# Attention with value parts side by side: denominators summed on GpSimd, the mask of the maxima put into the keys' sums

## The chip, the cores and the metric

The kernel runs on one core of a Trainium2 chip. The metric is the device time of one execution in microseconds (us); three executions of the kernel before took 2696.48, 2701.54 and 2703.55 us. Engines are called TensorE (PE; PEld is its weight load), VectorE (DVE), ScalarE (ACT), GpSimd (POOL) and SyncE (SP, which issues the loads).

## The reference

A two-layer decoder trunk on one sequence of 1024 tokens of width 1024, in float32. Layer 0 mixes tokens by attention with a forget gate (8 heads of 64) and by causal pooling, layer 1 by a recurrent delta rule (RWKV-7); a SwiGLU feed-forward block of width 2816 follows each. The change touches only the attention:

```python
logits = (jnp.einsum('bhqd,bhkd->bhqk', q_i, k).astype(jnp.float32) * scale
          + c_i[..., :, None] - cum[..., None, :])
causal = key_pos[None, :] <= q_pos[:, None]
p = jax.nn.softmax(jnp.where(causal, logits, -1e30), axis=-1)
return jnp.einsum('bhqk,bhkd->bhqd', p.astype(v.dtype), v)
```

`cum` is the running sum of the logarithm of the forget gate, so each key carries a number that is subtracted from its logits. The output of each head is then multiplied by a sigmoid gate.

## The kernel before

Matmuls take float32 operands rounded to a shorter form (`F32R`). To keep float32 accuracy an operand is split into a high part, rounded, and a low part, the rest; a product is then three matmuls: high by high, high by low, low by high (`mm3`, L163 to L165). ScalarE copies the high part, VectorE subtracts for the low one.

Everything is held transposed: channels or keys on the 128 partitions, tokens along the row, in halves of 512 tokens. Heads go in four pairs `p`, two heads `a` per pair; a head's 64 channels lie on its `own` half of the partitions, the `oth` half is free for other uses. For each head there are three steps:

- `assemble` splits the head's keys and queries into `KA`, `QA`, `KB`, `QB` and transposes its values (L490) into the high part `VH` (ScalarE, L492) and the low part `VL` (VectorE, L493). `VH` and `VL` have 128 columns per block of 128 keys: 64 for the head's values, and 64 others that were set once on GpSimd to ones in `VH` and to zeros in `VL`.
- `maxima` finds, for each query, the largest logit, so that the exponentials stay in range. It loads `cum` of the head, spread over all partitions, into `bc` (L500). For each block of 128 queries `i` from 0 to 7 and each half of the keys it makes the scores (L509), adds the causal mask in the diagonal block by a matmul of the identity with `maskQR` (L511), and VectorE subtracts `bc` and takes the largest (L512). The results go into rows of `QB`.
- `attend` makes, for each half `hq` of the queries and each block `j` of keys, the scores (L538, L539, mask L541 in the diagonal block), the exponentials `pt` (ScalarE, L543), their high part `ph` (ScalarE, the helper at L121) and low part `pl` (VectorE, L547), and one step later the values: `VH` by `ph` (L556), `VH` by `pl` (L557), `VL` by `ph` (L558), summed in one PSUM tile `o`. Since 64 columns of `VH` are ones, the `oth` half of `o` is the sum of the exponentials, the softmax's denominator. After the last `j`, ScalarE takes its logarithm (L563), VectorE adds the gate's logarithm (L564), ScalarE takes the exponential of the negative (L565), and VectorE multiplies (L566). A half has 4 or 8 blocks; widths are 512 columns, and 384, 256, 128 for the diagonal blocks that follow the first.

While a head is attended to, the next head is assembled and its maxima are found (`side`), and other matmuls fill TensorE: the projections of the next pair (`prep`), pooling units and gates, and for the last pair the output projection (`oproj_early`, which first splits 14 output tiles). `weave` interleaves these generators by the costs that they yield. A scheduler of the recording layer then sets each engine's order; each engine executes its own list in that order. Scratch tiles come from small rings: two PSUM tiles `s` for all scores, one `t`, two `o`, and five `tmp` tiles in SBUF that the pooling units, the heads' norms and the tail of `attend` share.

## Time and profile before

| | |
|---|---|
| median of 3 runs | 2701.54 us |
| profiled execution | 2699.03 us, its span 2697.2 us |
| TensorE busy, share of the span | 2633.8 us, 98% |
| VectorE | 1724.3 us, 64% |
| ScalarE | 1301.9 us, 48% |
| GpSimd | 50.6 us, 2% |
| first maxima to last values | about 72 to 466 us |
| two heads (pairs 0 to 2) | 101.3 us |

Busy time of TensorE is the union of matmuls that overlap: a 512-wide matmul lasts about 0.39 us in the records, and the next starts about 0.23 us after it. So the distance of starts, not the duration, is what a matmul costs. A stretch's bound is read from which engine has no idle time there and from what the others wait for.

### The profile page before, as it was taken

To read this page: it belongs to the slowest core of one execution; us is meant where nothing else is said; L and a number is where in the kernel's file an instruction comes from. 1 tells how busy PE (TensorE), PEld (TensorE's weight loads), DVE (VectorE), ACT (ScalarE), POOL (GpSimd) and SP (SyncE) were. 2 spreads that over 40 slices of the span, in tenths; PEclk is the share of its full clock that TensorE was granted. 3 is DMA by queue.
4 is the path that set the end of the run, shared out by engine and by line. 5 is a ranking of instruction groups with operands and counts; after the bars stand their busy time and mean duration, and the time that the engine had idled before them with its cause. 6 is when DMAs were issued, how large, how long until landed. Compare 5 with 4: busy or idle time off the path is not lost.

```text
span 2697.2 us, 40269 instructions
## 1 busy us (share of the span) xinstructions
PE 2633.8 (98%) x15368; PEld 2080.5 (77%) x15368; DVE 1724.3 (64%) x2940; ACT 1301.9 (48%) x2299; POOL 50.6 (2%) x139
## 2 busy tenths in 40 slices
PE   8999999999999999999999999999999999999999
PEld 6787878788888777777777677777777778888887
DVE  8777684654446655975995685469768856634443
ACT  7555564442224765534634466664445444332232
POOL 1000000000001000000000000000000000000000
PEclk9999999999999999999999999999999999999999
DMA  4111131233333546424523534454344336333333
GB/s 136 58 52 55 44 98 48 83 97 96 96 98 114 168 162 191 129 82 123 160 87 100 194 101 161 160 182 128 91 141 134 93 100 199 109 98 94 98 98 94
DMA packets 170817, 307.03 MB, mean 114 GB/s; under 512 B 18928, under 2 KB 25968, under 8 KB 170624
## 3 DMA queue, kind: packets, MB, share of 16 engines
q1 hardware_dynamic: 156800, 279.29, 33.6%
q10 hardware_dynamic: 13824, 25.17, 2.5%
q8 instruction: 120, 1.97, 0.3%
q14 instruction: 73, 0.60, 0.1%
HBM read 257.96 MB, written 46.43 MB: 113 GB/s over the span
## 4 chain that ended last, share of the span: by engine, by line
PE 77%; DVE 14%; DMA 3%; ACT 3%; issue 2%; SPq 0%; DVEq 0%; ACTq 0%
PE mm L163 16%; PE mm L164 16%; PE mm L165 16%; PE fm L163 6%; PE fm L164 5%; PE fm L165 5%; DVE wlo L152 2%; PE mm L175 1%; DVE nu L1108 1%; DVE pd L1106 1%; DMA wraw<-in_wu_dram 1%; DVE ZL L1064 1%; ACT whi L151 1%; PE o L1173 1%; PE s L1161 1%
## 5 line engine op out<-in xcount | busy, mean ns | idle before, releaser
L151 ACT CAST whi<-wraw 128x512 fp32r<-128x512 f32 x738 | 453.7, 617 | 867.4 <-PE mm L164 478.7
L152 DVE TENSOR_TENSOR wlo<-wraw,whi 128x512 fp32r<-128x512 f32 x738 | 501.3, 684 | 449.6 <-ACT whi L151 441.1
L163 PE MATMUL mm<-hh,whi 128*128 128x512 f32 x864 | 344.1, 400 | 6.2 <-ACT hh L355 6.1
L165 PE MATMUL mm<-hh,wlo 128*128 128x512 f32 x864 | 338.4, 392 | 0.0
L164 PE MATMUL mm<-hl,whi 128*128 128x512 f32 x864 | 337.9, 392 | 0.0
L163 PE MATMUL mm<-uh,whi 128*128 128x512 f32 x728 | 283.6, 391 | 0.9 <-DVE x L1317 0.9
L165 PE MATMUL mm<-uh,wlo 128*128 128x512 f32 x728 | 283.1, 390 | 1.0 <-DVE wlo L152 1.0
L164 PE MATMUL mm<-ul,whi 128*128 128x512 f32 x728 | 283.2, 390 | 0.0
L163 PE MATMUL fm<-h1h,whi 128*128 128x512 f32 x528 | 220.2, 417 | 14.8 <-DVE sg L726 9.9
L164 PE MATMUL fm<-h1l,whi 128*128 128x512 f32 x528 | 210.3, 398 | 0.1
L165 PE MATMUL fm<-h1h,wlo 128*128 128x512 f32 x528 | 209.5, 397 | 0.5 <-DVE wlo L152 0.5
L163 PEld LDWEIGHTS mm<-hh,whi 128*128 128x128 f32 x864 | 162.3, 188 | 43.4 <-ACT hh L355 7.8
L165 PEld LDWEIGHTS mm<-hh,wlo 128*128 128x128 f32 x864 | 162.5, 188 | 34.4 <-issue 0.2
L164 PEld LDWEIGHTS mm<-hl,whi 128*128 128x128 f32 x864 | 162.7, 188 | 33.1 <-DVE hl L260 1.7
L163 PE MATMUL fm<-hh,whi 128*128 128x512 f32 x416 | 170.9, 411 | 3.3 <-ACT hh L259 2.3
L164 PE MATMUL fm<-hl,whi 128*128 128x512 f32 x416 | 164.9, 396 | 0.2 <-DVE hl L260 0.2
L165 PE MATMUL fm<-hh,wlo 128*128 128x512 f32 x416 | 164.6, 396 | 0.0
L163 PEld LDWEIGHTS mm<-uh,whi 128*128 128x128 f32 x728 | 136.5, 188 | 34.6 <-issue 3.5
L164 PEld LDWEIGHTS mm<-ul,whi 128*128 128x128 f32 x728 | 136.6, 188 | 30.9 <-issue 1.1
L165 PEld LDWEIGHTS mm<-uh,wlo 128*128 128x128 f32 x728 | 136.7, 188 | 30.1 <-DVE wlo L152 1.8
L705 DVE TENSOR_TENSOR x<-mm,x 128x512 f32<-128x512 f32 x96 | 66.3, 692 | 119.3 <-PE mm L165 119.2
L163 PEld LDWEIGHTS fm<-h1h,whi 128*128 128x128 f32 x528 | 100.6, 191 | 47.1 <-DVE sg L726 12.2
(338 smaller groups left out, 4645.4 us busy)
## 6 DMA issues: line engine op xcount, KB each, us to landing
wraw<-in_wg_dram SPq DMA_DIRECT2D x176, 256.0 KB, 2.8
wraw<-in_wu_dram SPq DMA_DIRECT2D x176, 256.0 KB, 2.7
wraw<-in_wd_dram SPq DMA_DIRECT2D x176, 256.0 KB, 2.7
wraw<-in_w_in_dram SPq DMA_DIRECT2D x52, 256.0 KB, 2.9
x<-in_xT_dram SPq DMA_DIRECT2D x32, 256.0 KB, 4.6
x<-x SPq DMA_DIRECT2D x32, 256.0 KB, 3.3
wraw<-in_w_k_dram SPq DMA_DIRECT2D x32, 256.0 KB, 2.8
wraw<-in_w_v_dram SPq DMA_DIRECT2D x32, 256.0 KB, 3.0
```

The source lines that it names most:

```text
L151: k.nc.scalar.copy(hi[0:p, 0:n], raw[0:p, 0:n])
L152: k.nc.vector.tensor_tensor(lo[0:p, 0:n], raw[0:p, 0:n], rd(hi[0:p, 0:n]), ALU.subtract)
L163: nc.tensor.matmul(out, wh, xh, start=(first and i == 0), stop=False)
L164: nc.tensor.matmul(out, wh, xl, start=False, stop=False)
L165: nc.tensor.matmul(out, wl, xh, start=False, stop=(last and i == n - 1))
L175: k.nc.tensor.matmul(out[n * q:n * q + n], w[:, n * j:n * j + n], xs[j], start=c == 0, stop=c + g == len(xs), tile_position=(0, n * q))
L705: nc.vector.tensor_tensor(X[half][m], o, X[half][m], ALU.add)
L1064: nc.vector.tensor_tensor(ZL[h][HS[1 - h], i, bs], s4[HS[1]], self.msk[HS[1]].rearrange("p a t -> p (a t)").unsqueeze(1).broadcast_to([64, ...
L1106: nc.vector.tensor_tensor(pv, nu[:, j + 1:32, j:j + 1].broadcast_to([P, n, j]), nu[:, j:j + 1, 0:j].broadcast_to([P, n, j]), ALU.mult)
L1108: nc.vector.tensor_tensor(nu[:, j + 1:32, 0:j], nu[:, j + 1:32, 0:j], pv, ALU.add)
L1161: nc.tensor.matmul(z[HS[h], i], ZL[h][:, i, c, 0:64], SV[h][:, i, c], start=True, stop=True)
L1173: nc.tensor.matmul(sp[HS[h], i], BK[h][:, i, c], uv[h][:, i], start=True, stop=True)
```

## The change

Four things change.

- `VH` holds both parts side by side: the head's 64 `own` columns are the high part, the 64 `oth` columns the low part (VectorE writes it there). `VL` and the fills with ones and zeros are gone. Two matmuls remain per step, `VH` by `ph` and by `pl`; the `oth` half of `o` now holds the low part's products, and the two halves must be added at the end.
- The denominators: the exponentials of block `j = 0` are written into a tile `da`; for every further `j` GpSimd adds `pt` to it. At the end of a half, `finish` splits the sum into two parts (`part`: copy on ScalarE, subtraction on VectorE), copies the low half of `o` on ScalarE and adds it to the other half on VectorE, and then sums over the keys by two matmuls of `onesR` (all 1/64) with the two parts. Logarithm, gate, exponential and product follow as before. The tail takes four `tmp` tiles in place of one, and yields in two places, so that other work is woven in between.
- The maxima's mask matmuls are gone. GpSimd subtracts the mask from the diagonal block in `bc`, in place, so that the reduction on VectorE includes it.
- As the masked block stays masked, the blocks of queries go from the last to the first. `bc` has 512 more columns, a second copy of the first half of `cum` by a second load, so that query blocks 0 to 3 are masked there while blocks 4 to 7 read the unmasked first half.

```diff
-        nc.vector.tensor_tensor(VL[a][:, :, own], pvb, rd(VH[a][:, :, own]), ALU.subtract)
+        nc.vector.tensor_tensor(VH[a][:, :, oth], pvb, rd(VH[a][:, :, own]), ALU.subtract)
...
-        bc = ap_.tile([P, S], F32, tag="bc", name=nm(k, "bc"), bufs=1)
-        nc.sync.dma_start(bc, cumd[h:h + 1, :].broadcast_to([P, S]))
+        bc = ap_.tile([P, S + HN], F32, tag="bc", name=nm(k, "bc"), bufs=1)
+        nc.sync.dma_start(bc[:, 0:S], cumd[h:h + 1, :].broadcast_to([P, S]))
+        nc.sync.dma_start(bc[:, S:], cumd[h:h + 1, 0:HN].broadcast_to([P, HN]))
...
-        for i in range(8):
-            n = (i + 1) * P
-            for c in range(0, n, HN):
-                w = min(HN, n - c)
-                s = pst(k, "s", k.sbufs)
-                last = c + w == n
-                nc.tensor.matmul(s[:, 0:w], QA[a][:, P * i:P * i + P], KA[a][:, c:c + w], start=True, stop=not last)
-                if last:
-                    nc.tensor.matmul(s[:, w - P:w], identR, maskQR, start=False, stop=True)
-                nc.vector.tensor_tensor_reduce(s[:, 0:w], s[:, 0:w], bc[:, c:c + w], 1.0, -3e38, ALU.subtract, ALU.max,
-                                               mx[:, c // HN, i:i + 1])
-                yield w / HN + (0.5 if last else 0)
+        for i, c, at in [(i - d, c, at) for i in (7, 6, 5, 4) for d, c, at in ((0, HN, HN), (4, 0, S), (0, 0, 0))]:
+            w = min(HN, (i + 1) * P - c)
+            if at:
+                blk_ = bc[:, at + w - P:at + w]
+                nc.gpsimd.tensor_tensor(blk_, blk_, rd(maskQR), ALU.subtract)
+            s = pst(k, "s", k.sbufs)
+            nc.tensor.matmul(s[:, 0:w], QA[a][:, P * i:P * i + P], KA[a][:, c:c + w], start=True, stop=True)
+            nc.vector.tensor_tensor_reduce(s[:, 0:w], s[:, 0:w], bc[:, at:at + w], 1.0, -3e38, ALU.subtract, ALU.max,
+                                           mx[:, c // HN, i:i + 1])
+            yield w / HN + (0.5 if at else 0)
...
+            if j == 0:
+                pt = den[a, hq] = ap_.tile([P, HN], F32, tag="da", name=nm(k, "da"), bufs=2)
+            else:
+                pt = ap_.tile([P, HN], F32, tag="pt", name=nm(k, "pt"), bufs=2)
...
+            if j:
+                d = den[a, hq][:, q0 - hq * HN:]
+                nc.gpsimd.tensor_tensor(d, d, pt[:, 0:w], ALU.add)
...
-            nc.tensor.matmul(oo, VH[a][:, j], pl[:, 0:w], start=False, stop=False)
-            nc.tensor.matmul(oo, VL[a][:, j], ph[:, 0:w], start=False, stop=(j == nj - 1))
+            nc.tensor.matmul(oo, VH[a][:, j], pl[:, 0:w], start=False, stop=(j == nj - 1))
...
+            dh, dl = (ap_.tile([P, HN + 16], F32R, tag="tmp", name=nm(k, "dd"), bufs=k.tmpbufs)[:, 0:HN] for _ in range(2))
+            part(k, (dh, dl), d)
+            low = tmp("low")[:, 0:HN]
+            nc.scalar.copy(low[own], o[oth])
+            num = tmp("num")[:, 0:HN]
+            nc.vector.tensor_tensor(num[own], o[own], low[own], ALU.add)
+            yield 2
+            t = pst(k, "t", 1)
+            nc.tensor.matmul(t, onesR, dh, start=True, stop=False)
+            nc.tensor.matmul(t, onesR, dl, start=False, stop=True)
+            nc.scalar.activation(low[own], t[own], AF.Ln, scale=64.0)
+            nc.vector.tensor_tensor(low[own], low[own], y[p][hq][own], ALU.add)
+            nc.scalar.activation(low[own], low[own], AF.Exp, scale=-1.0)
+            nc.vector.tensor_tensor(y[p][hq][own], num[own], low[own], ALU.mult)
+            yield 0
...
             live.append(scores(*st))
             yield 2 * live[-1][4] / HN + 0.3
+            if ends and next(ends[0], None) is None:
+                ends.pop()
...
+        for e in ends:
+            yield from e
```

Three places in the engines' orders show what this moves. In these lists a line number is that of the kernel listed, so the change's numbers differ from the ones above: L537, L538 and L540 are its scores, L550 the low part `pl`, L553 the addition on GpSimd, L508 the mask on GpSimd, L562 and L563 the two value matmuls, L580 and L581 the two matmuls of `onesR`.

TensorE at the end of head 0, before: the last values, and the next head's first scores.

```order
L163 MATMUL mm_1268<-hh_392,whi_1219 128x512
L164 MATMUL mm_1268<-hl_393,whi_1219 128x512
L165 MATMUL mm_1268<-hh_392,wlo_1220 128x512
L556 MATMUL o_1072<-ph_1303,VH_109 128x128
L557 MATMUL o_1072<-pl_1304,VH_109 128x128
L558 MATMUL o_1072<-ph_1303,VL_111 128x128
L538 MATMUL s_1329<-QA_104,KA_102 128x512
L539 MATMUL s_1329<-QB_108,KB_106 128x512
L541 MATMUL s_1329<-maskTR,identR 128x128
```

The same place with the change (`dd` are the two parts of the denominators' sum):

```order
L165 MATMUL mm_1273<-hh_386,wlo_1226 128x512
L562 MATMUL o_1067<-ph_1308,VH_109 128x128
L563 MATMUL o_1067<-pl_1309,VH_109 128x128
L580 MATMUL t_1336<-dd_1326,onesR 128x512
L581 MATMUL t_1336<-dd_1327,onesR 128x512
L537 MATMUL s_1343<-QA_104,KA_102 128x512
L538 MATMUL s_1343<-QB_108,KB_106 128x512
L540 MATMUL s_1343<-maskTR,identR 128x128
```

The third product is gone, and the two matmuls of the denominators stand between the last values and the next head's scores, with no other matmul ahead of them. It is so for heads 0, 2 and 4.

VectorE at the same place with the change (`QA`, `KB`, `KA`, `QB` are assembly copies for a later head, `pl_1309` belongs to the last values above):

```order
L123 CAST KB_105<-ak_1135 64x512
L480 TENSOR_TENSOR KA_101<-ak_1135,KA_101 64x512
L484 TENSOR_TENSOR QB_107<-aq_1217,QA_103 64x512
L550 TENSOR_TENSOR pl_1309<-pt_1306,ph_1308 128x128
L260 TENSOR_TENSOR dd_1327<-da_1003,dd_1326 128x512
L441 TENSOR_TENSOR av_1334<-mm_1273,rs_98 128x512
L152 TENSOR_TENSOR wlo_1477<-wraw_1478,whi_1476 128x512
L577 TENSOR_TENSOR num_1332<-o_1067,low_1330 64x512
```

New are `dd_1327`, the low part of the sum, right behind the last `pl`, and `num_1332`, the addition of the two halves of `o`.

GpSimd with the change, during head 0, whose list held in this place only the small operations of the pooling units:

```order
L553 TENSOR_TENSOR da_838<-da_838,pt_981 128x128
L508 TENSOR_TENSOR bc_929<-bc_929,maskQR 128x128
L553 TENSOR_TENSOR da_1003<-da_1003,pt_1036 128x512
L508 TENSOR_TENSOR bc_929<-bc_929,maskQR 128x128 x2
L553 TENSOR_TENSOR da_1003<-da_1003,pt_1089 128x512
```

Additions for the head that is attended to and masks for the next head's maxima now take turns in one list.

More of the change, by code (lines that the diff above doesn't have):

```diff
@@ L381, in fox @@
     VH = [ap_.tile([P, 8, P], F32R, tag=f"VH{a}", name=f"VH{a}") for a in range(2)]
-    VL = [ap_.tile([P, 8, P], F32R, tag=f"VL{a}", name=f"VL{a}") for a in range(2)]
     for a in range(2):
@@ L388, in fox @@
         nc.gpsimd.memset(KB[a][64 - 64 * a:72 - 64 * a].bitcast(F32), 1.0)
-        nc.gpsimd.memset(VH[a][:, :, oth].bitcast(F32), 1.0)
-        nc.gpsimd.memset(VL[a][:, :, oth].bitcast(F32), 0.0)
     R = [K() for _ in range(4)]
@@ L395, in fox @@
     cumd = k.dram.tile([8, S], F32, tag="cum", name="cum")
-    cum = ap_.tile([P, S], F32, tag="bc", name="cum", bufs=1)[0:8]
+    cum = ap_.tile([P, S + HN], F32, tag="bc", name="cum", bufs=1)[0:8, 0:S]
     def forget(half, wf):
@@ L527, in attend @@
         steps = [(a, hq, j) for hq in range(2) for j in range(4 * hq + 4)]
-        live = []
-        out = {}
+        live, ends = [], []
+        out, den = {}, {}
         def scores(a, hq, j):
@@ L541, in scores @@
                 nc.tensor.matmul(s[:, 0:P], identR, maskTR, start=False, stop=True)
-            pt = ap_.tile([P, HN], F32, tag="pt", name=nm(k, "pt"), bufs=2)
+            if j == 0:
+                pt = den[a, hq] = ap_.tile([P, HN], F32, tag="da", name=nm(k, "da"), bufs=2)
+            else:
+                pt = ap_.tile([P, HN], F32, tag="pt", name=nm(k, "pt"), bufs=2)
             nc.scalar.activation(pt[:, 0:w], s[:, 0:w], AF.Exp, bias=ncumT[:, j, h:h + 1])
@@ L556, in values, with finish @@
             nc.tensor.matmul(oo, VH[a][:, j], ph[:, 0:w], start=(j == 0), stop=False)
-            nc.tensor.matmul(oo, VH[a][:, j], pl[:, 0:w], start=False, stop=False)
-            nc.tensor.matmul(oo, VL[a][:, j], ph[:, 0:w], start=False, stop=(j == nj - 1))
+            nc.tensor.matmul(oo, VH[a][:, j], pl[:, 0:w], start=False, stop=(j == nj - 1))
             if j == nj - 1:
-                own = slice(64 * a, 64 * a + 64)
-                oth = slice(64 - 64 * a, 128 - 64 * a)
-                den = tmp("den")[:, 0:HN]
-                nc.scalar.activation(den[own], o[oth], AF.Ln)
-                nc.vector.tensor_tensor(den[own], den[own], y[p][hq][own], ALU.add)
-                nc.scalar.activation(den[own], den[own], AF.Exp, scale=-1.0)
-                nc.vector.tensor_tensor(y[p][hq][own], o[own], den[own], ALU.mult)
-            return 3 * w / HN
+                ends.append(finish(a, hq, o, den[a, hq]))
+            return 3 * w / HN
+        def finish(a, hq, o, d):
+            own = slice(64 * a, 64 * a + 64)
+            oth = slice(64 - 64 * a, 128 - 64 * a)
+            dh, dl = (ap_.tile([P, HN + 16], F32R, tag="tmp", name=nm(k, "dd"), bufs=k.tmpbufs)[:, 0:HN] for _ in range(2))
[13 more added lines that the diff above has]
+            yield 0
         for st in steps:
```

## The prediction

> **What bounds the kernel now.** I read the page first, then the windows over the attention stage, then the timeline around the removed matmuls and around the end of a head.
>
> ```profile
> PE 2633.8 (98%) x15368; PEld 2080.5 (77%) x15368; DVE 1724.3 (64%) x2940; ACT 1301.9 (48%) x2299; POOL 50.6 (2%) x139
> ```
>
> TensorE is busy 98% of the span, GpSimd 2%. The stage that the change touches runs from the first maxima (72 us) to the last values (466 us). By windows:
>
> ```profile
> core 0: us, PE busy (x) PEld busy (x) DVE busy (x) ACT busy (x) POOL busy (x), PEclk, DMA share, GB/s
> 72.00:88.00 16.00, 15.04 (x72) 11.03 (x72) 14.52 (x38) 3.48 (x6) 0.64 (x3) 1.00 0.32 107
> 150.00:200.00 50.00, 48.95 (x236) 39.78 (x236) 34.38 (x73) 27.59 (x51) 2.25 (x4) 1.00 0.17 57
> 355.00:385.00 30.00, 28.54 (x137) 21.41 (x136) 28.13 (x59) 23.45 (x45) 0.40 (x4) 1.00 0.32 100
> 400.00:430.00 30.00, 30.00 (x145) 25.14 (x145) 14.94 (x29) 12.89 (x23) 0.00 (x0) 1.00 0.12 36
> ```
>
> The reader should see three kinds of stretch. From 88 to 355 us TensorE is full and VectorE is at about 70%; from 385 on TensorE is full and VectorE idles half the time. In 72 to 88 and 355 to 385 us VectorE is at 91 and 94%: there a VectorE microsecond decides, not a TensorE one. Busy time hides this, because the matmuls overlap; the count shows it: 236 matmuls per 50 us and 145 per 30 us, but only 137 per 30 us in the VectorE-bound stretch.
>
> **What a removed matmul is worth.** Starts of successive matmuls, not their durations, give the cost:
>
> ```profile
> 201.63 0.40 PE L557 MATMUL o<-pl,VH 128*128 128x512 f32 x1
> 201.87 0.40 PE L558 MATMUL o<-ph,VL 128*128 128x512 f32 x1
> 202.10 0.48 PE L277 MATMUL t<-ph,bones 128*128 128x512 f32 x1
> 202.42 0.22 PE L509 MATMUL s<-KA,QA 128*128 128x128 f32 x1
> ...
> 127.90 0.33 PE L558 MATMUL o<-ph,VL 128*128 128x384 f32 x1
> 128.07 0.39 PE L163 MATMUL mm<-hh,whi 128*128 128x512 f32 x1
> ...
> 130.72 0.28 PE L558 MATMUL o<-ph,VL 128*128 128x256 f32 x1
> 130.84 0.40 PE L163 MATMUL mm<-hh,whi 128*128 128x512 f32 x1
> ...
> 132.83 0.28 PE L558 MATMUL o<-ph,VL 128*128 128x128 f32 x1
> 132.95 0.45 PE L538 MATMUL s<-QA,KA 128*128 128x512 f32 x1
> ...
> 104.78 0.22 PE L511 MATMUL s<-maskQR,identR 128*128 128x128 f32 x1
> 104.84 0.44 PE L163 MATMUL mm<-hh,whi 128*128 128x512 f32 x1
> ```
>
> A 512-wide third product (L558) holds TensorE 0.23 us, a 384-wide one 0.17, a 256-wide and a 128-wide one 0.12 each, a mask matmul (L511) 0.06. There are 48, 16, 16 and 16 of L558: 48 x 0.23 + 16 x 0.17 + 32 x 0.12 = 17.6 us **removed**. The 64 mask matmuls: 64 x 0.06 = 3.8 us removed. **Added**: two 512-wide matmuls against the ones matrix for each of 8 heads and 2 query halves, 32 in all: 7.4 us at 0.23, or 10.2 us at the 0.32 that L277 above held TensorE, a matmul of the same kind that also stood for its operands. I take 7.4 and count such standing separately. Sum on TensorE: 17.6 + 3.8 - 7.4 = 14.0 us less (11.2 by the dearer end).
>
> Where VectorE decides this is not earned. The windows of L558 alone (first row) and of L511 alone (the other two) count it:
>
> ```profile
> 355.00:385.00 30.00, 3.59 (x10) 1.89 (x10) 1.00 0.32 100
> 355.00:385.00 30.00, 1.44 (x6) 1.14 (x6) 1.00 0.32 100
> 72.00:88.00 16.00, 1.39 (x6) 1.13 (x6) 1.00 0.32 107
> ```
>
> Ten third products (10 x 0.18, the mean of 17.6 / 96, is 1.8 us), twelve masks (0.7), and against them 4 of the new matmuls (0.9): 1.6 us are lost and **12.4 us** remain.
>
> **What VectorE and ScalarE get.** Per head and half the new tail adds, on VectorE, the low part of the denominator sums and the addition of the two value halves, and on ScalarE the copies of the sums and of the other half. The nearest rows (subtraction and copy of a 512-wide tile; I cost the operations on 64 partitions like them):
>
> ```profile
> L260 DVE TENSOR_TENSOR pl<-asq,ph 128x512 fp32r<-128x512 f32 x16 | 11.0, 686 | 0.3
> L259 ACT CAST ph<-asq 128x512 fp32r<-128x512 f32 x16 | 9.9, 616 | 0.6 <-PE o L558 0.5
> ```
>
> VectorE: 0.69 + 0.69 = 1.4 us, ScalarE two copies of 0.62, 1.2 us each time, 16 times. From 88 to 355 us this lies in the idle 15 us per 50 of VectorE and the 22 of ScalarE and I cost it at nothing; were the cover gone, it would be 1.4 us a time. In 355 to 385 us two such tails run (head 6's first half and its end): 2 x 1.4 = **2.8 us** on the path.
>
> How much lateness the rest can take is in the distance between a low part and its matmul:
>
> ```profile
> 203.00 0.69 DVE L547 TENSOR_TENSOR pl<-pt,ph 128x512 fp32r<-128x512 f32 x1 [0.17 <-ACT ph L121]
> 208.47 0.40 PE L557 MATMUL o<-pl,VH 128*128 128x512 f32 x1
> ...
> 372.65 0.44 PE L557 MATMUL o<-pl,VH 128*128 128x384 f32 x1 [0.41 <-DVE pl L547]
> ```
>
> Mid-head the low part is 4.8 us early; in the VectorE-bound stretch TensorE waits for it.
>
> **The ends of a head.** There the distance is also nil:
>
> ```profile
> 131.01 0.30 ACT L121 CAST ph<-pt 128x128 fp32r<-128x128 f32 x1
> 132.34 0.28 DVE L547 TENSOR_TENSOR pl<-pt,ph 128x128 fp32r<-128x128 f32 x1
> 132.67 0.33 PE L557 MATMUL o<-pl,VH 128*128 128x128 f32 x1 [0.21 <-DVE pl L547]
> 233.98 0.33 PE L557 MATMUL o<-pl,VH 128*128 128x128 f32 x1 [0.21 <-DVE pl L547]
> ```
>
> In the new order the two denominator matmuls stand right behind the last values at three head ends (heads 0, 2, 4; the place is shown in the section on the change); at the others and at all first halves other matmuls stand ahead of them. ScalarE's high copy can follow at 131.31 and end by 131.93; VectorE's low part then follows the last pl (132.62) and ends at 133.31. TensorE, after 0.12 for L557 and 0.23 for the first of the two, is free at 133.02: it stands 0.3 us, and everything behind it, the next head's scores first, stands with it. GpSimd's last addition must come before the high copy, so between 0 and 1.3 us each, 0.5 taken: 3 x 0.5 = **1.5 us**. At all 8 ends a GpSimd operation may also come between VectorE's assembly copies and the last pl: 0 to 0.4 each, 0.2 taken, **1.6 us**.
>
> **GpSimd.** Nothing in this trace adds two 512-wide tiles there. The nearest rows:
>
> ```profile
> L1091 POOL MEMSET XR<- 32x1024 f32 x8 | 7.6, 947 | 99.5 <-ACT XR L1061 99.5
> L389 POOL MEMSET VH<- 128x512 f32 x2 | 1.1, 527 | 0.1
> L1149 POOL COPY SV<-S 64x256 f32<-64x256 f32 x4 | 1.8, 450 | 141.5 <-PE o L1184 133.2 <-PE mm L164 8.1
> L609 POOL TENSOR_TENSOR x<-x,pu 128x16 f32<-128x16 f32 x4 | 1.2, 298 | 0.3
> 119.93 0.20 POOL L592 COPY pu<-halo 128x16 f32<-128x16 f32 x1 [40.45 <-DVE pl L260]
> 159.22 0.65 POOL L592 COPY pu<-halo 128x16 f32<-128x16 f32 x1
> 159.12 0.70 DVE L152 TENSOR_TENSOR wlo<-wraw,whi 128x512 fp32r<-128x512 f32 x1
> 864.99 1.37 POOL L773 COPY x<-hlast 128x1 f32<-128x1 f32 x1
> ```
>
> A head needs 10 additions (4 of 512, 2 each of 384, 256, 128: 3584 columns) and 8 masks of 128: 18 operations, 4608 columns. From below by the memsets, (947 - 527) / 512 = 0.82 ns a column, plus 0.2 us each: 3.8 + 3.6 = 7.4 us a head. From above by copies of one input, 0.20 us for 16 columns and 0.45 for 256, so 250 / 240 = 1.04 ns a column, taken twice for two inputs, with L609's 0.3 each: 9.6 + 5.4 = 15.0 us. I take about 11 us; a head lasts 50.6 us (132.67 to 233.98 is two heads), so GpSimd itself has room. The last four rows show the danger: the same 16-column copy takes 0.20 us alone and 0.65 us beside a VectorE operation that reads two SBUF tiles, and a one-column copy even 1.37. So the two engines keep each other waiting, and an addition of about 1 us would keep VectorE waiting longer than these tiny copies could show. In 355 to 385 us about 18 GpSimd operations fall: 0 to 6 us of VectorE, **1.5** taken.
>
> The Trainium skill's page "SBUF — State Buffer" (section "SBUF: two separate sides") speaks against the change here: a VectorE operation with two SBUF inputs and a GpSimd operation that reads SBUF share a port pair as an exclusive lock, for the whole instruction. The copies above agree from GpSimd's side; no row here shows VectorE's. The page "GPSIMD Engine Reference" (section "Elementwise — side-by-side cycle accounting") gives 4497 ns for an addition of 2048 columns, 2.2 ns a column; by it a head's GpSimd work would be an estimated 10.1 + 3.6 = 13.7 us, within my two ends.
>
> The masks also add a loop: a mask must wait until VectorE's previous reduction over the same half has read it, and the next reduction waits for the mask, with everything behind it on VectorE. Two other reductions (0.7 us each) lie between. The second load of the keys' sums goes through SP's queue right behind the first:
>
> ```profile
> 115.06 0.33 SPq L500 DMA_DIRECT2D bc<-cum  x1
> 140.65 0.28 PE L509 MATMUL s<-KA,QA 128*128 128x128 f32 x1
> ```
>
> 25 us early, so its 0.33 us is free. Only head 0's maxima, in 72 to 88 us, have nothing ahead: 0 to 2 us, **0.5** taken.
>
> **Sum**: -12.4 + 2.8 + 1.5 + 1.6 + 1.5 + 0.5 = -4.5 us against the profiled 2699.0 us, which is 2.5 us under the median of 2701.5. Carried over to the median: **2697 us**. With every cheap end: -12.4 + 2.8 = -9.6, 2692. With every dear end: -12.4 + 2.8 (dearer matmuls) + 2.8 + 3.9 + 3.2 + 6 + 2 = +8.3, 2710.
>
> **Rivals.** *TensorE earns it all* (faster). If VectorE in 355 to 385 us gains time because its order there is new, and GpSimd is near its low end, only the head ends remain: -14.0 + 1.5 = -12.5, 2689 us. For it: mid-head slack of 4.8 us. Against it: 94% VectorE.
>
> *GpSimd stops VectorE until VectorE is the bound* (slower). VectorE works 34.4 us per 50, so about 35 a head; with two tails 37.8. If it stood through all of GpSimd's 7.4 to 15.0 us, a head would need 45.2 to 52.8 us of it, against 50.6 now. The point that decides is 50.6 - 37.8 = 12.8 us of standing a head. At 15.0 us the six heads from 88 to 385 us grow by 2.2 us each and the matmuls' saving vanishes: 2701.5 + 13 = 2714 us. The 1.37 us row speaks for it; that many of VectorE's operations, all reductions of the maxima among them, read one input from PSUM speaks against.
>
> *The change earns nothing because scratch buffers tie the fill to the tails*: a tail takes four of five `tmp` tiles, so the pooling units that use the same five wait. At 0.5 us for each of 7 units 3.5 us: 2700 us, inside the forecast.
>
> **Chances.** This kernel's runs tell about 0.3% (8 us) from no change. Forecast with the third rival 0.45; the faster rival 0.34; the slower one 0.21. So faster 0.34, same 0.45, slower 0.21. The range takes in the faster rival with some scatter and most of the slower: 2686 to 2712; the forecast's own is 2692 to 2710.
>
> **What would show it.** L558 and L511 gone and the same 0.23 us between the remaining value matmuls; 32 new matmuls with waits of under 1 us at heads 0, 2 and 4; two heads in about 98 us instead of 101.3; VectorE still at 94% or more near 350 to 385 us, with that stretch 3 to 5 us longer; GpSimd at about 11 us a head. I am wrong if GpSimd's 512-wide addition takes over 1.5 us, if TensorE waits for reductions mid-head, or if the VectorE-bound stretch doesn't grow.

## The result and the profile after

| | before | after |
|---|---|---|
| median | 2701.6 us (4 runs, 2696.48 to 2703.55) | 2718.5 us (4 runs, 2716.25 to 2723.39) |
| profiled execution, span | 2699.0, 2697.2 us | 2718.3, 2716.5 us |
| last product of a low part, head 7 (L557, now L563) starts at | 464.7 us | 482.3 us |

The change is slower: after / before is 1.0068 (95% interval 1.0054 to 1.0082), and 2718.5 lies outside the predicted 2686 to 2712. What follows that product takes 2232.5 us before and 2234.2 after in the profiled executions, so the loss is inside the stage. The page's line of busy times after:

```profile
PE 2627.5 (97%) x15240; PEld 2060.8 (76%) x15240; DVE 1783.3 (66%) x2972; ACT 1316.2 (48%) x2331; POOL 172.9 (6%) x279
```

TensorE has 128 matmuls and 6 us less (160 removed, 32 added). VectorE has 59 us more for 32 more instructions, which explain 22 us (32 x 0.69). The other 37 us are old instructions that got longer. The groups of VectorE over the stage (line, operation, out<-in, shape and count, then busy us and mean ns of one), first before:

```profile
L152 DVE TENSOR_TENSOR wlo<-wraw,whi 128x512 fp32r<-128x512 f32 x56 | 38.4, 687 | 16.4 <-ACT whi L151 15.6 <-PE s L539 0.3
L512 DVE CUSTOM_DVE_ANT_0 s<-s,bc 128x512 f32<-128x512 f32 x48 | 33.3, 705 | 4.0 <-PE s L511 2.5 <-PE s L509 1.2
L547 DVE TENSOR_TENSOR pl<-pt,ph 128x512 fp32r<-128x512 f32 x48 | 33.0, 687 | 12.4 <-ACT ph L121 11.9
L482 DVE TENSOR_TENSOR KA<-ak,KA 64x512 fp32r<-64x512 f32 x14 | 9.6, 686 | 0.5 <-ACT KA L481 0.2
L123 DVE CAST QA<-aq 64x512 fp32r<-64x512 f32 x14 | 5.9, 422 | 0.4
```

and after:

```profile
L152 DVE TENSOR_TENSOR wlo<-wraw,whi 128x512 fp32r<-128x512 f32 x57 | 45.3, 800 | 9.8 <-ACT whi L151 9.7
L511 DVE CUSTOM_DVE_ANT_0 s<-s,bc 128x512 f32<-128x512 f32 x48 | 33.3, 696 | 15.8 <-PE s L510 15.6
L550 DVE TENSOR_TENSOR pl<-pt,ph 128x512 fp32r<-128x512 f32 x32 | 28.7, 896 | 5.5 <-ACT ph L121 5.2
L480 DVE TENSOR_TENSOR KA<-ak,KA 64x512 fp32r<-64x512 f32 x14 | 12.3, 879 | 0.4
L550 DVE TENSOR_TENSOR pl<-da,ph 128x512 fp32r<-128x512 f32 x16 | 11.0, 689 | 2.6 <-ACT ph L121 2.6
L577 DVE TENSOR_TENSOR num<-o,low 64x512 f32<-64x512 f32 x16 | 11.0, 685 | 1.4 <-ACT low L575 1.0
L123 DVE CAST QA<-aq 64x512 fp32r<-64x512 f32 x14 | 8.8, 631 | 0.4
```

Read these by operands. Longer are the operations whose inputs are all in SBUF: the low parts of the weights and probabilities, the assembly, the casts. Unchanged are the reduction of scores (`s` is in PSUM) and the sum `num` (`o` is in PSUM). Also unchanged is `pl<-da`, the low part of block 0, when GpSimd has nothing to add. GpSimd's groups in the stage after:

```profile
L553 POOL TENSOR_TENSOR da<-da,pt 128x512 f32<-128x512 f32 x32 | 44.4, 1389 | 75.5 <-ACT pt L546 69.8 <-DVE pl L550 5.7
L508 POOL TENSOR_TENSOR bc<-bc,maskQR 128x128 f32<-128x128 f32 x64 | 41.9, 657 | 61.9 <-DVE mx L511 37.7 <-DMA bc<-cum 23.9
L553 POOL TENSOR_TENSOR da<-da,pt 128x384 f32<-128x384 f32 x16 | 17.0, 1063 | 45.6 <-ACT pt L546 37.7 <-DVE low L583 5.0 <-DVE pl L550 2.8
L553 POOL TENSOR_TENSOR da<-da,pt 128x256 f32<-128x256 f32 x16 | 12.1, 755 | 39.1 <-ACT pt L546 38.9
L553 POOL TENSOR_TENSOR da<-da,pt 128x128 f32<-128x128 f32 x16 | 8.6, 535 | 27.8 <-ACT pt L546 27.7
```

Together 124.0 us, 15.5 a head. The largest waits of TensorE (PE) and of its weight loads (PEld) between 88 and 466 us (engine, line, waited for: us in total, times, longest), after:

```profile
PEld s L510 <- DVE mx L511: 9.9, 15, 2.7
PEld o L563 <- DVE pl L550: 8.7, 18, 1.1
PEld t L278 <- DVE pl L260: 5.4, 8, 1.7
PE s L510 <- DVE mx L511: 5.4, 5, 2.3
PE t L517 <- DVE m L515: 5.3, 7, 0.9
```

Before, the largest of that view was 4.1 us:

```profile
PEld o L557 <- DVE pl L547: 4.1, 11, 0.6
```

One place shows the mechanism. The timeline after, around 269 us, has start, duration, engine:

```profile
268.05 0.69 DVE L625 TENSOR_TENSOR pb<-pa 128x525 f32<-128x525 f32 x1
...
268.76 0.50 PE L510 MATMUL s<-KA,QA 128*128 128x512 f32 x1
...
268.85 1.74 POOL L553 TENSOR_TENSOR da<-da,pt 128x512 f32<-128x512 f32 x1 [1.89 <-ACT pt L546]
269.49 1.65 DVE L625 TENSOR_TENSOR pa<-pb 128x521 f32<-128x521 f32 x1
...
271.07 0.42 DVE L511 CUSTOM_DVE_ANT_0 s<-s,bc 128x256 f32<-128x256 f32 x1
...
271.41 0.13 DVE L511 DVE_READ_ACCUMULATOR2_ANT mx<- 128x1 f32 x1
...
271.60 0.47 PE L510 MATMUL s<-KA,QA 128*128 128x128 f32 x1 [2.34 <-DVE mx L511]
```

VectorE starts a pooling addition of two inputs in SBUF at 269.49 (its like at 268.05 took 0.69 us), while GpSimd adds denominators from 268.85 to 270.59. It takes 1.65 us, 0.96 more; 269.49 + 0.96 is 270.45, about GpSimd's end. The reduction behind it is late, it frees the scores' tile late, and TensorE idles for 2.34 us.

By the Trainium skill's "SBUF — State Buffer", section "SBUF: two separate sides", the first of two such operations takes the shared ports for its whole instruction and the other waits. The trace agrees, with 0.96 us of standing here.

### The profile page after: what moved, and what is told of

It reads as the page before. It is cut to its first block, busy times and chain, and to the rows that moved or that the text cites. A ratio compares the mean times of both kernels' runs of the same rounds, so it can differ in the third digit from the quotient of the medians.

```text
span 2716.5 us, 40347 instructions
## 1 busy us (share of the span) xinstructions
PE 2627.5 (97%) x15240; PEld 2060.8 (76%) x15240; DVE 1783.3 (66%) x2972; ACT 1316.2 (48%) x2331; POOL 172.9 (6%) x279
## 4 chain that ended last, share of the span: by engine, by line
PE 73%; DVE 16%; DMA 4%; ACT 4%; issue 3%; SPq 0%; POOL 0%; DVEq 0%; ACTq 0%
PE mm L163 16%; PE mm L164 15%; PE mm L165 15%; PE fm L163 6%; PE fm L164 5%; PE fm L165 5%; DVE wlo L152 3%; PE mm L175 1%; DMA wraw<-in_wd_dram 1%; DVE nu L1131 1%; DVE pd L1129 1%; DVE ZL L1087 1%; ACT whi L151 1%; DMA y<-y 1%; PE o L1196 1%
## 5 line engine op out<-in xcount | busy, mean ns | idle before, releaser
L152 DVE TENSOR_TENSOR wlo<-wraw,whi 128x512 fp32r<-128x512 f32 x738 | 507.8, 693 | 445.2 <-ACT whi L151 435.9
L163 PEld LDWEIGHTS fm<-h1h,whi 128*128 128x128 f32 x528 | 100.5, 191 | 49.8 <-DVE sg L749 14.6
```

The costliest lines, as they stand in the source:

```text
L152: k.nc.vector.tensor_tensor(lo[0:p, 0:n], raw[0:p, 0:n], rd(hi[0:p, 0:n]), ALU.subtract)
L163: nc.tensor.matmul(out, wh, xh, start=(first and i == 0), stop=False)
```

## The experiments

Times are medians, beside the kernel before on the same chip (2701 to 2703 us in each batch). What follows the stage took 2228 to 2248 us in the profiled executions (span less the time of that last product; mean granted clock 0.987 to 0.995), so a median can carry a few us that the stage did not make; the longest (2247.5) had a clock of 0.987, the shortest (2228.5) 0.995. So I also give **S**: how much later than before the last head's last product of a low part starts in the profiled execution. S is one execution each; two kernels that should be equal there, without GpSimd's work and with memsets in its place, differ by 0.1 us. It is less sure elsewhere: with the free ends S is 2.9 us later than with the additions alone, while the median is 1.9 us lower. S also carries stretches at half clock inside the stage (last section): up to 5.1 us in the change, 3.4 with exponentials in PSUM and casts on ScalarE, and 1.7 in the paced additions, three `pt` tiles, free ends and additions a step later. Kernels without additions or masks leave out a part of the result.

| kernel | median | ratio to before (95%) | S |
|---|---|---|---|
| after | 2718.5 | 1.0068 (1.0054 to 1.0082) | +17.6 |
| no work on GpSimd | 2689.1 | 0.9947 (0.9926 to 0.9967) | -13.6 |
| idle additions, unpaced | 2728.8 | 1.0087 (1.0067 to 1.0108) | |
| idle memsets, unpaced | 2691.7 | 0.9959 (0.9944 to 0.9974) | |
| idle additions, paced | 2703.7 | 1.0010 (1.0000 to 1.0019) | +0.7 |
| memsets, paced | 2688.3 | 0.9947 (0.9930 to 0.9963) | -13.5 |
| masks alone on GpSimd | 2695.7 | 0.9975 (0.9966 to 0.9984) | -7.1 |
| additions alone on GpSimd | 2715.0 | 1.0054 (1.0039 to 1.0069) | +6.9 |
| the same, no additions | 2704.3 | 1.0011 (1.0000 to 1.0022) | -3.4 |
| the same, three `pt` tiles | 2715.2 | 1.0040 (1.0021 to 1.0060) | +7.7 |
| the same, free ends | 2713.1 | 1.0051 (1.0034 to 1.0068) | +9.8 |
| exponentials in PSUM | 2711.1 | 1.0030 (1.0017 to 1.0044) | +5.2 |
| the same, no additions | 2700.8 | 0.9993 (0.9982 to 1.0003) | -1.6 |
| the same, casts on ScalarE | 2712.1 | 1.0035 (1.0024 to 1.0046) | +8.1 |
| additions on VectorE | 2709.5 | 1.0022 (1.0010 to 1.0034) | +3.4 |
| the same, a step later | 2709.3 | 1.0017 (1.0008 to 1.0026) | +1.5 |
| the same, casts on ScalarE | 2703.1 | 1.0004 (0.9991 to 1.0017) | -2.8 |
| the same, casts and more tiles | 2700.9 | 0.9996 (0.9983 to 1.0009) | -2.9 |
| before, casts on ScalarE | 2697.0 | 0.9978 (0.9968 to 0.9988) | -2.4 |

Theories: **C**, GpSimd's reading of SBUF holds VectorE, and TensorE waits for what comes late; **E**, the new ends of the query halves take the time; **H**, the hand-over: results of GpSimd come late.

### Without GpSimd's work

```diff
-                nc.gpsimd.tensor_tensor(blk_, blk_, rd(maskQR), ALU.subtract)
-                nc.gpsimd.tensor_tensor(d, d, pt[:, 0:w], ALU.add)
-            nc.scalar.activation(low[own], t[own], AF.Ln, scale=64.0)
+            nc.scalar.activation(low[own], t[own], AF.Ln, bias=1.0, scale=64.0)
```

> The change without GpSimd's work: neither the additions of the denominators nor the subtraction of the mask is done, so the denominators are those of the first key block alone and the maxima run over unmasked keys (1 is added ahead of the logarithm so that it stays finite); everything else of the change is kept. Theory C (GpSimd's additions with two operands in SBUF hold VectorE's operations that read SBUF, and TensorE waits for the reductions and low parts that come late): the wait goes, and what is left is the prediction's sum without its GpSimd terms, 2690 to 2698 us; the 512-column low part of a probability falls back from 896 to about 690 ns, and VectorE from 1783 to about 1745 us. Rival E (the new ends of the query halves, parts of the denominators, numerators and their product, take the time): 2714 to 2719. Rival H (hand-over: what waits for a result of GpSimd comes late, the reductions for the mask and the parts for the last addition): 2690 to 2698 as well, so this run parts E from the other two.

2689.1 us: 29.4 us below the change, 31.2 in S. (The last line keeps the logarithm finite; it is the same wherever additions are left out.) E falls: the ends are all there, and cost next to nothing. The windows from 88 us to the last such product (columns: window and length, then busy us and instructions of TensorE, its weight loads, VectorE, ScalarE and GpSimd, the granted clock, DMA). Before:

```profile
88.00:464.70 376.70, 371.00 (x1781) 301.57 (x1781) 255.82 (x528) 212.69 (x391) 7.92 (x24) 1.00 0.18 56
```

Without GpSimd's work:

```profile
88.00:451.10 363.10, 355.61 (x1657) 282.22 (x1656) 275.13 (x561) 225.01 (x422) 7.32 (x24) 1.00 0.21 64
```

After:

```profile
88.00:482.30 394.30, 368.26 (x1655) 284.18 (x1654) 315.80 (x573) 226.15 (x422) 128.08 (x162) 0.99 0.20 59
```

TensorE's work falls by 15.4 us and its idle time (window less busy) only goes from 5.7 to 7.5: that is the -13.6. With GpSimd's work the idle time is 26.0, 18.5 more, and the same matmuls keep TensorE busy for 12.7 us more: at most 5.1 of these are half clock, and the rest I put down, by argument alone, to matmuls that no longer overlap behind a wait. For VectorE these windows don't compare, since the last holds 12 operations more that slipped behind 88 us. Counted from the start of the execution the operations are the same, first without GpSimd's work, then after:

```profile
0.00:451.10 451.10, 436.82 (x2000) 340.52 (x2001) 348.73 (x698) 283.00 (x524) 14.51 (x42) 1.00 0.25 77
0.00:482.30 482.30, 449.56 (x2000) 342.55 (x2001) 386.84 (x697) 283.97 (x524) 139.24 (x186) 0.99 0.23 72
```

VectorE's operations take 38.1 us more (386.84 against 348.73).

### Idle additions and memsets

In the kernel without GpSimd's work:

```diff
             if j:
+                nc.gpsimd.tensor_copy(tick, pt[:, 0:1])
+                nc.gpsimd.tensor_tensor(junk[:, 0:w], junk[:, 0:w], junk[:, 0:w], ALU.add)
```

> The kernel without GpSimd's work, to which GpSimd gets as many additions of the same widths at the same places (one per key block after the first, started by that block's probabilities), but of a tile with itself, whose result nobody reads: the same time on GpSimd, no hand-over. Denominators and masks are left out as in the kernel without GpSimd's work. Theory C: two thirds of GpSimd's standing (10.3 of 15.5 us per head) come back and with them about two thirds of the loss, 2707 to 2715 us, and the low parts go to 850 ns or more. Rival H: nobody waits for these additions, so the same as without GpSimd's work within 3 us. Rival E: 2714 to 2719, the same as without GpSimd's work.

> As the idle additions, but each is replaced by three memsets of the same width on the same tile (about the same time on GpSimd, 3 x 0.53 us for 512 columns by the start's memsets of 527 ns, with no operand read). Denominators and masks are left out as there. Theory C, in the form that it is the reading of two SBUF operands by GpSimd that holds VectorE: the same as without GpSimd's work within 3 us (2690 to 2700), the low parts about 690 ns. If any GpSimd instruction holds VectorE, or GpSimd's late release of the probabilities' tile does it: 2707 to 2715, as the idle additions. Rival E: 2714 to 2719.

2728.8 and 2691.7 us. Nothing tied these to their place: the junk tile does not depend on the copy, and the trace has the additions between 7 and 98 us, the memsets between 7 and 123. So the two numbers say nothing on the place of the change. They do compare the two kinds of work at the start, where VectorE is busy 77.87 of 95 us with the memsets: 80 additions cost 39.7 us there (in part by the clock, which was granted at 0.91 in these 95 us), 240 memsets 2.6. The next pair copies into the first column of `junk`, so that each addition waits for its block:

```diff
-                nc.gpsimd.tensor_copy(tick, pt[:, 0:1])
+                nc.gpsimd.tensor_copy(junk[:, 0:1], pt[:, 0:1])
```

> The idle additions again, now bound to their place: the first element of the idle tile is copied from the probabilities of each key block after the first, and the addition of the tile with itself reads it, so each addition runs where the change has its own, and nobody waits for the result. Denominators and masks are left out as in the kernel without GpSimd's work. Theory C: that kernel's 2689 and about two thirds of the 29 us by which the change is above it (82 of its 124 us on GpSimd are additions), 2704 to 2714; the operations of VectorE that have two operands in SBUF get longer, the reductions of scores in PSUM stay at 0.70 us for 512. Rival H (late hand-over of GpSimd's results): 2687 to 2694, as nothing is handed over.

> The same with three memsets of the same width in place of each addition, bound to their place in the same way; denominators and masks left out as there. Theory C: no operand is read, so nothing is held, 2687 to 2696. If the late release of the probabilities' tile or any work on GpSimd at these places did it: as the paced additions.

2703.7 us and 2688.3 us: 14.6 us for the additions, none for the memsets. H cannot make these 14.6 us, since nobody waits for the results. With the additions, the low parts among VectorE's groups and the additions among GpSimd's:

```profile
L547 DVE TENSOR_TENSOR pl<-pt,ph 128x512 fp32r<-128x512 f32 x32 | 30.1, 940 | 5.8 <-ACT ph L121 5.6
L508 DVE CUSTOM_DVE_ANT_0 s<-s,bc 128x512 f32<-128x512 f32 x48 | 33.3, 696 | 15.0 <-PE s L507 14.9
```

```profile
L550 POOL TENSOR_TENSOR junk<-junk 128x512 f32<-128x512 f32 x32 | 39.2, 1226 | 2.5
```

With the memsets:

```profile
L547 DVE TENSOR_TENSOR pl<-pt,ph 128x512 fp32r<-128x512 f32 x32 | 22.0, 688 | 7.1 <-ACT ph L121 6.9
```

```profile
L551 POOL MEMSET junk<- 128x512 f32 x96 | 50.5, 526 | 5.5
```

GpSimd is busy longer with the memsets (three times 526 ns against 1226) and VectorE doesn't notice. What holds VectorE is not that GpSimd works; what the additions do and the memsets don't is read wide tiles from SBUF. (The copies of one column, 80 in both kernels, read SBUF too, and cost nothing that shows.)

### The two parts apart

Masks alone (the additions left out):

```diff
-                nc.gpsimd.tensor_tensor(d, d, pt[:, 0:w], ALU.add)
```

> The change without the additions (the denominators are those of the first key block alone, with 1 added ahead of the logarithm), the subtraction of the mask kept on GpSimd. 42 of 124 us of GpSimd's work are left. Theory C: a third of the 29 us, 2694 to 2702. Rival H by the masks: 2710 or more; by the last addition: 2689.

Additions alone (maxima and their order as in the kernel before):

```diff
-                nc.gpsimd.tensor_tensor(blk_, blk_, rd(maskQR), ALU.subtract)
+                    nc.tensor.matmul(s[:, w - P:w], identR, maskQR, start=False, stop=True)
```

> The change with the masks as products on TensorE, as before, and the additions on GpSimd; the result is the reference's. Theory C: the paced additions' time and the masks' 3.8 us, and up to 4 us for the parts that wait for the last addition: 2707 to 2720. Rival H with the masks as its hand-over (reductions that wait for a subtraction behind additions in GpSimd's queue): 2693 to 2699.

2695.7 us, 6.6 more than without GpSimd's work (6.5 in S), inside the range of C and under its third of 9.8. Of the 6.5, 1.9 are there by the end of head 0, whose maxima start 3.1 us later, after the first masks (first reduction at 80.79 against 77.67 us); this looks like hand-over or order, not like holding. No idle masks were tried, so what holding and hand-over share of the rest is not shown. And 2715.0 us. I first read this as 22 us for the additions, over 2689 and 3.8 for the masks' products, 7.5 more than the idle ones cost, and looked for a hand-over in the release of `pt` and in the ends that wait for the last addition:

```diff
-                pt = ap_.tile([P, HN], F32, tag="pt", name=nm(k, "pt"), bufs=2)
+                pt = ap_.tile([P, HN], F32, tag="pt", name=nm(k, "pt"), bufs=3)
```

> The denominators on GpSimd and masks on TensorE (2715.0) with three tiles for the probabilities in place of two, so that an exponential does not wait until GpSimd has added the tile from two blocks earlier. If the 7.5 us by which the real additions cost more than the idle ones are this release: 2707 to 2711. If they are VectorE's waits or the ends that wait for the last addition: 2713 to 2717.

```diff
-                ends.append(finish(a, hq, o, den[a, hq]))
+                ends.append(finish(a, hq, o, still))
```

> The denominators on GpSimd, masks on TensorE (2715.0), the same additions of the same tiles, but the ends of the query halves take their parts from a tile of ones that was set once, and nobody reads the sums (so the denominators are left out of the result). If the 7.5 us by which the real additions cost more than the idle ones are the ends that wait for the last addition and what stands behind them on VectorE and ScalarE: 2706 to 2710. If the real additions hold VectorE more than the idle ones: 2713 to 2717.

2715.2 and 2713.1 us: neither. The base was wrong, as the run without additions shows:

```diff
-                nc.gpsimd.tensor_tensor(d, d, pt[:, 0:w], ALU.add)
```

> The denominators on GpSimd and masks on TensorE (2715.0) without the additions (denominators of the first key block alone, with 1 added ahead of the logarithm); the masks and the order of the maxima's products are those of the kernel before. If the masks' products and the old order of the maxima cost no more than the products' 3.8 us above the kernel without GpSimd's work: 2691 to 2695, and the real additions cost 22 us. If they cost more together: 2698 to 2702, and the real additions cost the 14.6 us of the idle ones.

2704.3 us. So the real additions cost 10.7 us there (10.3 in S), less than the idle ones in the new order, and no hand-over is needed. Instead the masks' products and the old order of the maxima cost 15.2 us (10.2 in S), not 3.8. The windows of this kernel:

```profile
88.00:461.30 373.30, 364.43 (x1720) 291.63 (x1719) 274.18 (x560) 226.90 (x422) 7.06 (x24) 1.00 0.18 56
```

Against the kernel without GpSimd's work it has 63 matmuls and 8.8 us of TensorE more in this window: 0.14 a mask. The timeline before shows why 0.06 was too little:

```profile
104.78 0.22 PE L511 MATMUL s<-maskQR,identR 128*128 128x128 f32 x1
104.84 0.44 PE L163 MATMUL mm<-hh,whi 128*128 128x512 f32 x1
105.12 0.40 PE L164 MATMUL mm<-hl,whi 128*128 128x512 f32 x1
```

The 512-wide matmul behind the mask holds TensorE for 0.28 us (0.29 in the median of the 64 places), not 0.23. The mask's line in the trace before has its weight load (ns, shortest, median and longest):

```profile
L511 PEld LDWEIGHTS s<-maskQR,identR x64: 187/188/192, 68.3 to 404.1; 128*128 128x128 f32 x64
```

A load lasts 0.19 us, a mask only 0.06, so the next weights are not there in time (argued from these durations). With the 0.06 of the mask that is 0.12 a mask, 7.7 us for 64. How the rest divides between masks and order wasn't tried.

### Probabilities in PSUM

```diff
-                pt = ap_.tile([P, HN], F32, tag="pt", name=nm(k, "pt"), bufs=2)
+                pt = s
-                nc.gpsimd.tensor_tensor(d, d, pt[:, 0:w], ALU.add)
+                nc.gpsimd.tensor_tensor(d, d, rd(ph[:, 0:w]), ALU.add)
```

> The denominators on GpSimd, the masks on TensorE (as in the run of the denominators alone, 2715 us), but the probabilities of all key blocks after the first stay in the scores' PSUM tile: the exponential is written there, the high part is copied from there and the low part is PSUM less high part; GpSimd adds the high parts (so the denominators leave out the low parts of these blocks). The additions on GpSimd are the same in number, width and place, but the low parts now have one operand in PSUM. Theory C (only VectorE's operations with both operands in SBUF are held): the low part of 512 columns falls from 983 to about 690 ns, and with it some two thirds of the 22 us that the additions cost there, 2698 to 2707 us. Rival H (GpSimd's late results themselves): still 2711 to 2719. The scores' tile is held longer by the copy and the low part, which could cost some us; the same kernel without additions measures that.

> The same without the additions on GpSimd (denominators of the first key block alone, with 1 added ahead of the logarithm): the masks' 3.8 us on TensorE above the kernel without GpSimd's work, 2693, and what the longer held scores' tile costs, 0 to 8 us: 2690 to 2701.

2711.1 and 2700.8 us, so the additions cost 10.3 us (6.8 in S) where they cost 10.7 (10.3) with `pt` in SBUF. Groups of VectorE with PSUM and additions:

```profile
L152 DVE TENSOR_TENSOR wlo<-wraw,whi 128x512 fp32r<-128x512 f32 x57 | 43.4, 768 | 11.7 <-ACT whi L151 11.3
L549 DVE TENSOR_TENSOR pl<-s,ph 128x512 fp32r<-128x512 f32 x32 | 21.9, 686 | 5.8 <-ACT ph L121 5.3
L260 DVE TENSOR_TENSOR pl<-asq,ph 128x512 fp32r<-128x512 f32 x13 | 10.9, 839 | 3.5 <-ACT ph L259 3.5
```

The mechanism is confirmed: beside the same additions the low part is back at 686 ns, from 983. The gain I expected is not. VectorE's time grows by 10.8 us with the additions (347.21 to 358.04, from the start to the last such product), less than half of the 23.5 with `pt` in SBUF, and yet S and the median gain little: a part of the holding moved to operations still in SBUF, the weights' low parts (768 ns; 711 with `pt` in SBUF, 685 without additions) and the norms' (839; 707; 684).

```diff
-    CE="VVA"
+    CE="AAA"
```

With the casts on ScalarE too:

> The exponentials in PSUM and the additions on GpSimd (2711.1), with the two casts of queries and keys on ScalarE too. The casts read SBUF and write SBUF on VectorE and grew by up to half in the change (0.42 to 0.63 us for the queries'). Theory C: less of what GpSimd can hold is left on VectorE, 2701 to 2707. If what is left of the cost is hand-over or the weights' low parts: 2708 to 2713.

2712.1 us: nothing gained. The casts were not what remained; beside these additions they took 422 and 436 ns on VectorE, against 422 undisturbed.

### Additions on VectorE

```diff
-                nc.gpsimd.tensor_tensor(d, d, pt[:, 0:w], ALU.add)
+                nc.vector.tensor_tensor(d, d, pt[:, 0:w], ALU.add)
```

> The change with the additions on VectorE in place of GpSimd and the masks as products on TensorE as before; the result is the reference's. VectorE gets 12 additions per head, 3584 columns, about 5.3 us per head or 42 in all by the undisturbed low parts (0.69 us for 512), which is no less than the 37 us by which its operations were stretched in the change; TensorE has 3.8 us of mask products more than the change. Theory C: VectorE is as full as in the change but its operations come in order and none stands for long, so 2698 to 2712. Rival E: 2718 to 2724. Rival H: 2692 to 2700, no hand-over is left and 5.3 us per head of 33 lie beside TensorE.

2709.5 us, S +3.4: 5.2 us above the kernel with masks on TensorE and no additions (6.8 in S). From the start to the last such product, without the additions and with them on VectorE:

```profile
0.00:461.30 461.30, 444.52 (x2064) 348.27 (x2065) 347.91 (x698) 284.69 (x524) 13.93 (x42) 1.00 0.22 70
0.00:468.10 468.10, 450.00 (x2064) 347.61 (x2065) 383.32 (x778) 285.34 (x524) 15.30 (x42) 1.00 0.22 69
```

VectorE does 35.4 us more (347.91 to 383.32, 80 operations) and the stage gets 6.8 us longer, 0.19 for each. Holding was dearer. The same with the paced idle additions, with the masks alone and with the additions alone:

```profile
0.00:465.40 465.40, 442.25 (x2000) 339.86 (x2001) 372.75 (x698) 283.43 (x524) 109.53 (x203) 1.00 0.24 74
0.00:457.70 457.70, 440.14 (x2001) 339.59 (x2001) 354.27 (x698) 282.66 (x524) 54.53 (x106) 1.00 0.24 76
0.00:471.70 471.70, 449.30 (x2065) 348.03 (x2065) 371.42 (x697) 286.77 (x524) 95.04 (x122) 1.00 0.22 69
```

VectorE's time there (third pair) against the kernels without that work (348.73, and 347.91 where the masks are on TensorE):

| | VectorE longer by | S later by | for each |
|---|---|---|---|
| additions, old order | 23.5 | 10.3 | 0.44 |
| paced idle additions | 24.0 | 14.3 | 0.60 |
| masks alone | 5.5 | 6.5 | 1.18 |
| the change | 38.1 | 31.2 | 0.82 |
| additions on VectorE | 35.4 | 6.8 | 0.19 |

The masks' row need not be holding alone, as said above. A us of VectorE's own work cost less than half of what a us of holding did. Why was not measured; a reading is that a held operation has those that TensorE needs queued behind it. Next, whether order or load makes the 6.8 us; the additions a step later:

```diff
-            if j:
-                d = den[a, hq][:, q0 - hq * HN:]
-                nc.vector.tensor_tensor(d, d, pt[:, 0:w], ALU.add)
...
         def values(a, hq, j, q0, w, ph, pl, pt):
+            if j:
+                d = den[a, hq][:, q0 - hq * HN:]
+                nc.vector.tensor_tensor(d, d, pt[:, 0:w], ALU.add)
```

> The additions on VectorE, each written one step later, behind the next block's low part, with a third tile for the probabilities. If the order costs: 2696 to 2704. If the load costs: 2707 to 2712.

The casts on ScalarE (`CE="AAA"`) with the additions on VectorE, then with more tiles, then alone in the kernel before:

> The additions on VectorE (2709.5 us) and the two casts of queries and keys, 0.42 us each and four per head, moved from VectorE to ScalarE: VectorE loses 1.7 us per head, a third of what the additions put there. If VectorE's load is what costs there: 2698 to 2706. If it is the order (an addition ahead of a low part or a reduction that TensorE waits for): 2706 to 2711.

```diff
-    k.tmpbufs=5
+    k.tmpbufs=6
-                pt = ap_.tile([P, HN], F32, tag="pt", name=nm(k, "pt"), bufs=2)
+                pt = ap_.tile([P, HN], F32, tag="pt", name=nm(k, "pt"), bufs=3)
```

> The additions on VectorE and the casts on ScalarE (2703.1), with a third tile for the probabilities and a sixth for the short-lived tiles, in the room that the low values left. If tiles bind there: 2696 to 2701, faster than both kernels. If VectorE's load does: 2701 to 2705.

> The kernel before, with the two casts of queries and keys moved from VectorE to ScalarE and nothing else: whether the 6 us that this move earned with the additions on VectorE (2709.5 to 2703.1) come from room on VectorE that the additions had used up. If so, the kernel before, whose VectorE is not that full, stays within 4 us of its 2701, or is slower since a ScalarE cast delays an exponential. If the move is good in itself: 2693 to 2697.

2709.3 us a step later (that kernel also has a third `pt` tile): by the median order isn't it, though S is 1.9 us less. 2703.1 with the casts on ScalarE and 2700.9 with more tiles, S the same in both. The casts alone, in the kernel before, give 2697.0 us (5.5 less, 2.4 in S) against 6.4 (6.2) with the additions on VectorE, so by the medians the move is good in itself, and room on VectorE explains at most the difference in S. At 0.9978 (0.9968 to 0.9988) that is the one complete kernel here that beats both, and it owes nothing to the change.

## Why the prediction was wrong

**The step that failed** is the one that costed VectorE's waiting between 88 and 355 us at nothing and let GpSimd hold it only "In 355 to 385 us", at 1.5 us (0 to 6). Measured: GpSimd's work costs 29.4 us in all, 31.2 in S. By place, from the kernel without GpSimd's work to the change, the lateness grows by 4.8 us in head 0, then by 3.3, 2.9, 8.9, 3.4, 5.4, 2.4 and nothing in head 7. Head 0 has the first masks in it (below); 18.6 us come in heads 1 to 4, where VectorE was idle 30% of the time, and 7.8 in heads 5 and 6, around 355 to 385 us. That cover was a mean: a low part that comes 4.8 us early mid-head doesn't help a reduction whose scores' tile TensorE needs at once. The prediction did see the danger in a 16-column copy of 0.65 us beside a VectorE operation, but priced it for VectorE in that one stretch only.

**T1, TensorE.** -14.0 forecast, -15.4 measured, by two errors. The values part earned 6.6 us (371.00 to 364.43), not 10.2: if the 17.6 holds, a matmul of `onesR` costs 0.34, above the dear 0.32. The masks earned 8.8 in place of 3.8, since the forecast counted the distance behind a mask and not that behind the next matmul. The 1.6 us said to be lost where VectorE decides, the tails' 2.8, the exposed ends' 1.5 and the last low parts' 1.6, 7.5 in all, came to 1.8 us of idle TensorE without GpSimd's work (7.5 less 5.7). So these terms were too dear, and "TensorE earns it all", 2689 us, is what the kernel without GpSimd's work gives: 2689.1. That it fits so well is partly luck, since the two errors largely cancel.

**GpSimd's own time** was taken at 11 us a head and is 15.5, above the dear end of 15.0. By the shortest of each kind in the change (1.27, 1.00, 0.73 and 0.46 us for 512, 384, 256 and 128 columns, 0.46 for a mask) a head is 13.1 us, so 2.1 of the 4.5 are the price and 2.4 GpSimd's own standing: a mask takes 657 ns in the mean.

**First masks**: 0.5 (0 to 2). Head 0's first product of a low part starts at 97.5 us with the masks on GpSimd, at 92.5 without GpSimd's work: 5.0 us, of which 1.9 are left by the end of that head with the masks alone.

**The slower rival** had the right side and nearly the size (2714), but another condition: a bound reached at 12.8 us of standing a head. The change stretches VectorE by 38.1 / 8 = 4.8 us a head, and VectorE is at 80% of the window (315.80 of 394.30). So the loss came without that bound being reached. **The rival of the scratch tiles** falls with the kernel without GpSimd's work, which has the same tails.

**The signs**: "TensorE waits for reductions mid-head" was named as what would prove me wrong, and came (9.9 us in 15 waits). GpSimd's 512-wide addition stayed at 1.39 us, under the 1.5 named. The VectorE-bound stretch grew as forecast (3 to 5 us): head 5, which has it, took 43.5 us in place of 39.8. Two heads took 104.7 us, where about 98 was forecast.

**Not settled**: idle additions and masks alone sum to 20.8 us in S, the change has 31.2. Of the 10.4, VectorE's stretch is 8.6 us larger than the sum (38.1 against 24.0 + 5.5), at the rates of the additions and of the change (0.60 and 0.82) an estimated 5 to 7 us; half clock takes at most 3.4 more (5.1 against 1.7). Additions and masks share GpSimd's list, and what that adds was not tried alone; the waits that the trace of the change puts down to GpSimd sum to 3.8 us, all of ScalarE. Nor was late hand-over tried in the full change, only for the additions in the old order.

## What to carry to other kernels

An engine with 6% of the span can still set the time: ask what memory its instructions read, and which operations of the busy engine read the same. Work for GpSimd beside a busy VectorE should read nothing from SBUF (memsets were free), and moving one VectorE operand to PSUM frees that operation but can pass a part of the holding to others. Idle share is no cover for a stall that falls inside a chain; test a suspected contention with idle work that nobody waits for, and measure the base with everything but that one thing.

## What was not expected of the hardware

A short gap on TensorE can cost its clock. After the 2.34 us at 269 us, the windows of the change show:

```profile
268.00:270.00 2.00, 1.21 (x5) 0.42 (x3) 1.94 (x4) 1.19 (x2) 1.15 (x1) 1.00 0.33 123
270.00:272.00 2.00, 0.40 (x2) 0.40 (x3) 2.00 (x4) 1.50 (x4) 0.96 (x2) 0.74 0.00 0
272.00:274.00 2.00, 2.00 (x6) 1.61 (x6) 1.94 (x4) 0.34 (x1) 1.02 (x2) 0.50 0.00 0
274.00:276.00 2.00, 2.00 (x7) 1.52 (x6) 1.17 (x5) 0.00 (x0) 0.00 (x0) 0.50 0.00 0
276.00:278.00 2.00, 2.00 (x8) 1.57 (x7) 1.08 (x4) 0.45 (x1) 0.00 (x0) 0.55 0.00 0
278.00:280.00 2.00, 2.00 (x11) 1.65 (x10) 1.95 (x4) 1.48 (x3) 0.89 (x2) 1.00 0.00 0
```

About 6.8 us at half clock: at most 3.4 us lost behind a wait of 2.3. It came again for 3.4 us near 295 us, where TensorE idles 1.9 us of 6 with no gap over 0.9, and in the paced idle additions behind a gap of 2.10 us; but not in the change behind five single gaps of 1.3 to 1.5 us. The length of a gap does not decide by itself. With the exponentials in PSUM and the casts on ScalarE half clock came near 268 and 391 us behind gaps of 1.31 us with shorter ones beside them, with three `pt` tiles near 388 us behind a single gap of 1.30, and with the additions a step later it came near 382 us with no gap over 0.9. In each case in the stage TensorE had been idle for 1.3 to 2.1 of the 3.4 us ahead of it (1.74 ahead of the stretch shown); the change also has such a stretch that was idle for 1.44 us, up to 165 us, and kept the clock. So these runs give no single limit. The Trainium skill, "TensorE: Matmul & The Clock Gate", section "Why this matters for your kernels", allows gaps up to about 3 us. Here 2.3 and 2.1 were enough, and once 1.3.
